# Changing the size of the first load, and with it the partition pitch, in a max-pooling kernel bound by its loads

## The chip, the cores and the metric

The kernel runs on one core of one Trainium2 chip. The metric is the device time of a run in microseconds (us); medians of several runs are given. The span in a profile is the same execution without what surrounds it, about 1.7 us less. On one core there is no second die to compare with, and all runs quoted here counted as fast runs, at a granted clock of 1.00.

## The reference

The reference takes x of 32 x 256 x 4096 float32 and gives 32 x 256 x 256: each output is the maximum of 16 neighbouring inputs.

```
for i in range(output_size):                 # 256
    start = int(i * length / output_size)    # 16 * i
    end = int((i + 1) * length / output_size)
    result[:, :, i] = np.max(x[:, :, start:end], axis=-1)
```

So 134.2 MB are read, 8.4 MB are written, and there is one operation: a maximum over windows of W = 16 elements (64 B). Each of the 128 partitions handles 16,384 windows.

## The kernel before

A partition reads consecutive windows from the input. The windows come in two groups; within a group, partition p starts p x (windows of the group) x 64 B behind the group's first byte. That distance is called the *pitch* here. One buffer, `ring`, has two halves, each with a gap of 152 windows, so that a load can be issued when the larger part (872 windows) of the reduction before it in the same half is done. The results go to a second buffer, `kept`, and leave at the end in two *kept stores*, one for each group. The results of the last load alone go to a free part of `ring` and leave in a transfer of their own, the *small store*, which ScalarE issues when the last reduction is done.

```
CHUNK = 1024
GAP = 152
FIRST = 132
LOADS_A, LOADS_B = 9, 6
last = total - FIRST - (LOADS_A + LOADS_B) * CHUNK      # 892
...
for g, loads in enumerate(
    ([FIRST] + [CHUNK] * LOADS_A, [CHUNK] * LOADS_B + [last])
):
    xg, og = group(sum(loads))       # [128 partitions, windows of the group]
    a = 0
    for n in loads:
        xn = xg[:, a * W : (a + n) * W]
        ...                          # FIRST goes into the gap, the rest:
        low = n_loads % 2 * (CHUNK + GAP)
        moved = n_loads // 2 % 2
        at = low + moved * GAP
        nc.sync.dma_start(out=ring[:, at * W : (at + n) * W], in_=xn)
        if n == CHUNK:
            cut = CHUNK - GAP if moved else GAP
            parts = [(0, cut), (cut, n)]
            for u, v in parts if moved else parts[::-1]:
                pooled(dst[:, u:v], at + u, v - u)     # reduce_max into kept
        else:
            end = (at + CHUNK) * W
            last_kept = ring[:, end - n : end]
            pooled(last_kept, at, n)
        ...
nc.scalar.dma_start(out=og[:, full : full + last], in_=last_kept)
tc.no_sync_barrier()
for dst, src in stores:              # one kept store for each group
    nc.sync.dma_start(out=dst, in_=src)
```

## Time and profile before

| | before |
|---|---|
| first three runs, median (lowest to highest) | 335.11 us (334.94 to 335.2) |
| span of the profiled run | 333.4 us |
| VectorE busy | 276.5 us, 83% |
| rate of an 8 MB load in the steady part | 433.5 GB/s |
| VectorE idle before each 8 MB load's reduction | 2.07 us |

The page's part on DMA issues, below, has in its columns the tile written and read, the issuing queue, the count, the size, and the time from issue to landing. In all profile lines DVE is VectorE, which does the reductions; SPq and ACTq are the queues of SyncE and ScalarE, which issue the transfers.

### The profile page before, as it was taken

The numbers are of one execution on the slowest core, as the hardware profiler recorded it, in microseconds if no ns is written. First come the engines' busy times: TensorE is split into PE (matmuls) and PEld (weight loads), VectorE is DVE, ScalarE is ACT, GpSimd is POOL, SyncE is SP. The second block draws the span as 40 slices with busy tenths as digits, with TensorE's granted clock in tenths as the row PEclk, the third lists the DMA queues.
The fourth block names the chain that finished last, engine by engine and source line by source line (L and its number), as shares of the span: only waits on it lengthen the run. The fifth ranks groups of instructions, "written<-read, shape, count | busy, mean of one in ns | idle before, by whom it ended". The sixth has DMA issues, their size and how long they took to land.

```text
span 333.4 us, 113 instructions
## 1 busy us (share of the span) xinstructions
DVE 276.5 (83%) x32; POOL 0.2 (0%) x4
## 2 busy tenths in 40 slices
DVE  2009979797997979799797979979797997979993
POOL 0000000000000000000000000000000000000000
DMA  9898989999898989999898989999898989899997
GB/s 381 377 503 377 495 385 480 401 401 480 377 503 377 503 377 480 401 393 488 377 503 377 503 377 480 401 425 456 377 503 377 503 377 495 385 455 438 397 402 317
DMA packets 2880, 142.61 MB, mean 428 GB/s; under 512 B 320, under 2 KB 320, under 8 KB 448
## 3 DMA queue, kind: packets, MB, share of 16 engines
q1 hardware_dynamic: 2736, 142.15, 98.7%
q10 hardware_dynamic: 144, 0.46, 0.3%
HBM read 134.22 MB, written 8.39 MB: 428 GB/s over the span
## 4 chain that ended last, share of the span: by engine, by line
DMA 58%; DVE 36%; DVEq 5%; issue 0%; SPq 0%
DMA ring<-in_x_dram 58%; DVE kept L52 36%; DVEq L143 5%; SPq L83 0%
## 5 line engine op out<-in xcount | busy, mean ns | idle before, releaser
L52 DVE TENSOR_REDUCE kept<-ring 128x872 f32<-128x13952 f32 (+2 forms) x31 | 261.5, 8477 | 51.8 <-DMA ring<-in_x_dram 51.8
L52 DVE TENSOR_REDUCE ring<-ring 128x892 f32<-128x14272 f32 x1 | 15.0, 15009 | 0.0
L129 POOL MEMSET const-bfloat16-1.0<- 128x1 bf16 x1 | 0.1, 102 | 0.0
L129 POOL MEMSET const-uint8-127<- 128x1 uint8 x1 | 0.1, 102 | 0.0
L129 POOL MEMSET const-float32-1.0<- 128x1 f32 x1 | 0.1, 99 | 0.0
L129 POOL MEMSET const-float32-0.0<- 128x1 f32 x1 | 0.1, 98 | 0.2 <-issue 0.2
## 6 DMA issues: line engine op xcount, KB each, us to landing
ring<-in_x_dram SPq DMA_DIRECT2D x1, 7136.0 KB, 21.5
out_dram<-kept SPq DMA_DIRECT2D x1, 4674.0 KB, 32.2
out_dram<-kept SPq DMA_DIRECT2D x1, 3072.0 KB, 18.0
ring<-in_x_dram SPq DMA_DIRECT2D x1, 1056.0 KB, 5.1
out_dram<-ring ACTq DMA_DIRECT2D x1, 446.0 KB, 4.2
ring<-in_x_dram SPq DMA_DIRECT2D x15, 24.0
```

Of the source, the lines that this page charges most:

```text
L52: nc.vector.reduce_max(out=dst, in_=ring[:, at * W : (at + n) * W].rearrange("p (n w) -> p n w", w=W), axis=mybir.AxisListType.X,)
L129: nc = _bacc.Bacc("TRN2", target_bir_lowering=False, num_devices=1)
L143: with _tile.TileContext(nc) as tc:
```

## The change

The first load becomes 128 windows, exactly 8 KB per partition, in place of 132 (8448 B). That alone would make the pitch of the first group an even number of 256 B (9344 x 64 = 2336 x 256 B), so the ninth 8 MB load is made 4 windows, 256 B, shorter: 2335 x 256 B. The last load takes the 8 windows left over, 900 in place of 892.

```
-    FIRST = 132
+    FIRST = 128
     LOADS_A, LOADS_B = 9, 6
-    last = total - FIRST - (LOADS_A + LOADS_B) * CHUNK
+
+    LESS = 4
+    group_a = [FIRST] + [CHUNK] * (LOADS_A - 1) + [CHUNK - LESS]
+    last = total - sum(group_a) - LOADS_B * CHUNK
+    group_b = [CHUNK] * LOADS_B + [last]
 ...
-    for g, loads in enumerate(
-        ([FIRST] + [CHUNK] * LOADS_A, [CHUNK] * LOADS_B + [last])
-    ):
+    for g, loads in enumerate((group_a, group_b)):
 ...
-                if n == CHUNK:
+                if n != last:
```

## The prediction

> **What bounds the kernel now.** I read the page's shares first, then the memory line, then the chain of waits, then the DMA queue's own waits, and last the stretches of the start and the end. The page says which resource is full:
>
> ```profile
> DVE 276.5 (83%) x32; POOL 0.2 (0%) x4
> DMA packets 2880, 142.61 MB, mean 428 GB/s; under 512 B 320, under 2 KB 320, under 8 KB 448
> q1 hardware_dynamic: 2736, 142.15, 98.7%
> HBM read 134.22 MB, written 8.39 MB: 428 GB/s over the span
> ```
>
> VectorE has 17% of slack, the DMA queue of SyncE has 1.3%. The reads are exactly the input (134.22 MB) and the writes exactly the output (8.39 MB), so no byte can be saved. The packet count also tells how a transfer is cut. There are 17 loads and 3 stores of 128 partitions, 20 x 128 = 2560 packets, and 20 x 16 = 320 small ones (the "under 512 B" group, the completion signals); together 2880. So each partition's run, 64 KB long or 8448 B long, is one packet.
>
> The chain of waits in order of time alternates between loads and reductions. Three of its pieces in the middle and all from the last wait on:
>
> ```profile
> 25.17 14.70 DVE kept L52
> 39.87 0.02 issue
> 39.88 23.97 DMA ring<-in_x_dram
> ...
> 272.09 23.96 DMA ring<-in_x_dram
> 296.06 0.02 issue
> 296.08 16.89 DVE kept L52 x2
> 312.97 0.09 issue
> 313.06 15.23 DVEq L143
> ```
>
> That looks as if each 14.7 us reduction were on the path, since the load is issued only when it ends. It is not. The 8 MB load issued at 39.88 needs only 19.35 us of transfer, yet takes 23.97 us, so it stands 4.6 us in the queue behind the load before it. VectorE's lines of the timeline near the end give that period, and the slack on the other side:
>
> ```profile
> 257.38 17.28 DVE L52 TENSOR_REDUCE kept<-ring 128x872 f32<-128x13952 f32 x2 [2.07 <-DMA ring<-in_x_dram]
> 276.74 17.28 DVE L52 TENSOR_REDUCE kept<-ring 128x872 f32<-128x13952 f32 x2 [2.08 <-DMA ring<-in_x_dram]
> 296.08 17.28 DVE L52 TENSOR_REDUCE kept<-ring 128x872 f32<-128x13952 f32 x2 [2.06 <-DMA ring<-in_x_dram]
> 313.27 15.01 DVE L52 TENSOR_REDUCE ring<-ring 128x892 f32<-128x14272 f32 x1
> ```
>
> Starts lie 19.35 us apart, work is 17.28 us, VectorE idles 2.07 us a round. A load of 128 x 65536 B = 8,388,608 B in 19.35 us is 433.5 GB/s: the loads run back to back at one rate and set the pace. At the end two paths nearly meet. VectorE goes on without a pause (296.08 + 17.28 = 313.36) into the last reduction and is done at 328.28, after which the last small store takes 4.2 us to land. The DMA engines meanwhile do the other two stores. The stretches show that they have no hole either:
>
> ```profile
> core 0: us, DVE busy (x) POOL busy (x), PEclk, DMA share, GB/s
> 5.86:8.21 2.35, 2.35 (x1) 0.00 (x0) 1.00 1.03 446
> 8.21:25.17 16.96, 0.00 (x2) 0.00 (x0) 1.00 1.00 433
> 25.17:313.27 288.10, 259.10 (x30) 0.00 (x0) 1.00 1.00 431
> 313.27:328.28 15.01, 15.01 (x2) 0.00 (x0) 1.00 1.01 436
> 328.28:333.36 5.08, 0.00 (x1) 0.00 (x0) 1.00 0.59 245
> ```
>
> The fourth row is the last reduction: DMA share 1.01, full, with stores of the kept results. In the trace's packet records the last kept-store packet ends 1.1 us before the last packet of the small store. So the span is: some 1.7 us until the first packet, 330.25 us in which the engines always have packets, and 1.4 us of receipt and closing. The timed run adds about 1.7 us to the span (335.11 against 333.4).
>
> **What the Trainium skill says.** "DMA: Bandwidth & Descriptors", section "Where 436 GB/s comes from", puts the ceiling of the 16 engines' way into SBUF at 435.2 GB/s. The trace agrees: 433.5 GB/s in the steady part, so no better layout in HBM can win more than 0.4%. The same page, section "How a descriptor splits into AXI transactions", says that a run aligned to 256 B is cut into transactions of 256 B and a remainder. The old first run is 8448 B = 33 x 256, the new one 8192 B = 32 x 256, and both start on a 256 B boundary (every load starts at a multiple of 4 windows of 64 B). By that section 8448 B has no remainder to lose; the trace shows it as one packet and at best 319 ns, 16 x 8448 / 319 = 424 GB/s, so hardly worse than a long one. The same page's "Latency and other measured facts" has a row on HBM row pitches at large powers of two that halve the rate; nothing of the kind is to be seen in this trace. "VectorE: DVE Perf Modes", in its perf-mode table, has tensor_reduce at 1x in fp32 only, with a clock of 0.96 GHz: 872 x 16 elements would be an estimate of 14.53 us, the trace has 14.69. So a window of 16 costs 16.8 ns (15,009 ns / 892).
>
> **The change part by part.** No operation is added or removed: 32 reductions, 17 loads, 3 stores as before, with the same waits in the built program. Only four sizes move.
>
> (1) First load 132 to 128 windows per partition. Removed: 128 x 256 B = 32,768 B, at 433.5 GB/s 0.076 us. The first reduction starts perhaps 0.08 us earlier and is 4 x 16.8 = 67 ns shorter. It has 16.96 us of idle time behind it, so nothing reaches the end from VectorE.
> (2) Ninth 8 MB load 1024 to 1020 windows: again 0.076 us less transfer, and its big reduction 872 to 868 windows, 67 ns less, in front of an idle 2.07 us. Hidden.
> (3) The last load takes what the two gave up, 892 to 900 windows: 65,536 B more, +0.151 us. Sum of the loads: -0.076 - 0.076 + 0.151 = 0.00 us, so the last load lands when it did. The load before it lands 0.15 us earlier.
> (4) The last reduction is 8 x 16.8 = 0.135 us longer. VectorE's tail: start of the last 17.28 us pair 0.151 us earlier, last reduction 0.135 us longer, sum -0.016 us. It ends at about 328.26 instead of 328.28, provided that the last load is there when VectorE becomes free. It lands at about 313.06 and VectorE comes free at 313.27 - 0.15 = 313.12: just in time; were it 0.1 us late, VectorE would end at 328.36. The small store grows from 3568 to 3600 B a partition, 4 KB or 0.01 us, and a kept store shrinks by as much.
>
> The pitch between partitions of the first group goes from 9348 x 64 = 598,272 B = 2337 x 256 B to 9340 x 64 = 597,760 B = 2335 x 256 B; of the second group from 7036 x 64 = 1759 x 256 B to 7044 x 64 = 1761 x 256 B. All four are odd, and counted in units of 8 KB they lie one 256 B step above or below a whole number (2336 = 73 x 32, 1760 = 55 x 32): the two groups only swap sides. I expect the same rate. Total: 0.00 us for the bytes, -0.02 to +0.1 us for the tail.
>
> **The rivals.** (a) *The start gains.* The first load needs 3.7 us from first to last packet where the steady rate would need 2.5, and single packets take up to 1186 ns. If exactly 8 KB avoided some of that, up to 1.2 us could go: 333.9. For it: those long packets. Against it: they are only the earliest ones, later packets of the same load take 319 ns, which is what start-up looks like, not a cost per packet. I give it one chance in ten for a part, 0.3 us. (b) *The pitch changes the rate.* If 2335 and 1761 suited HBM worse, the 8 MB packets, now about 2418 ns, would lengthen; 1% is 3.2 us: 338.3. Against it: mirror-image pitches. For it: somebody took pains to keep it odd. (c) *The last wait changes hands.* VectorE waits for the last load instead of for itself: at most +0.1 us: 335.2. Plausible, and hardly measurable beside a spread of 0.26 us between three runs. (d) *VectorE's tail gains because the work is better spread.* It cannot: the DMA queue is full to the end on its own.
>
> **Range and chances.** Bytes, packets and operations are the same, so the middle is 335.11 less a few hundredths, with a small pull from (a): 335.05. The three runs spread over 334.94 to 335.20; adding (a) and (c), and a different hour or chip, gives 334.6 to 335.6 for 8 in 10. To gain 2% (6.7 us) the 142.61 MB would have to go through in 330.25 - 6.7 = 323.5 us, that is at 441 GB/s where they now take 432, above anything steady here; to lose as much needs rival (b) at double size. Faster 0.01, same 0.98, slower 0.01.
>
> **What would show it right or wrong.** Right: the page again has 2880 packets, 142.61 MB and 428 GB/s; reductions of 8 MB loads start 19.35 us apart, except 0.08 us less around the ninth; the last reduction is about 15.14 us and begins about 313.1; the queue's share stays near 98.7%. Step (1) is wrong if the first reduction starts earlier than 5.5 us and the whole chain shifts with it. Rival (b) shows as a period other than 19.35 us; rival (c) as idle time before the last reduction. The prediction as a whole fails if the long packets' rate moves by even half a per cent, or if the packet count changes.

## More of the kernel before

The large times contain time in the queue, as the prediction works out for an 8 MB load.

```profile
ring<-in_x_dram SPq DMA_DIRECT2D x1, 7136.0 KB, 21.5
out_dram<-kept SPq DMA_DIRECT2D x1, 4674.0 KB, 32.2
out_dram<-kept SPq DMA_DIRECT2D x1, 3072.0 KB, 18.0
ring<-in_x_dram SPq DMA_DIRECT2D x1, 1056.0 KB, 5.1
out_dram<-ring ACTq DMA_DIRECT2D x1, 446.0 KB, 4.2
ring<-in_x_dram SPq DMA_DIRECT2D x15, 24.0
```

## The result, and the profile after

| | before | after |
|---|---|---|
| median of 6 runs each (lowest to highest) | 334.96 us (334.92 to 335.2) | 334.87 us (334.78 to 335.01) |
| ratio | | 0.9996, 95% interval 0.9984 to 1.0009 |
| span of the profiled run | 333.4 us | 333.2 us |

A ratio is the mean time of one kernel's fast runs over that of the other's of the same rounds, so it isn't quite the ratio of the two medians.

The page of the changed kernel, its parts on bytes and queues:

```profile
DVE 276.5 (83%) x32; POOL 0.2 (0%) x4
DMA packets 2880, 142.61 MB, mean 428 GB/s; under 512 B 320, under 2 KB 320, under 8 KB 448
q1 hardware_dynamic: 2736, 142.15, 98.8%
HBM read 134.22 MB, written 8.39 MB: 428 GB/s over the span
```

Packets, bytes and mean rate are those of before. VectorE's timeline of the changed kernel, its first two and last four lines (start, duration, operation, count, and the idle time ahead of it):

```profile
5.40 2.29 DVE L56 TENSOR_REDUCE kept<-ring 128x128 f32<-128x2048 f32 x1 [5.40 <-DMA ring<-in_x_dram]
24.75 17.28 DVE L56 TENSOR_REDUCE kept<-ring 128x872 f32<-128x13952 f32 x2 [17.07 <-DMA ring<-in_x_dram]
...
257.06 17.28 DVE L56 TENSOR_REDUCE kept<-ring 128x872 f32<-128x13952 f32 x2 [2.08 <-DMA ring<-in_x_dram]
276.41 17.28 DVE L56 TENSOR_REDUCE kept<-ring 128x872 f32<-128x13952 f32 x2 [2.07 <-DMA ring<-in_x_dram]
295.75 17.28 DVE L56 TENSOR_REDUCE kept<-ring 128x872 f32<-128x13952 f32 x2 [2.07 <-DMA ring<-in_x_dram]
312.95 15.14 DVE L56 TENSOR_REDUCE ring<-ring 128x900 f32<-128x14400 f32 x1
```

The period is still about 19.35 us (19.36 in the mean; single starts lie 19.24 to 19.47 us apart), and the last reduction took 15.14 us without idle time before it. But the whole column lies 0.22 to 0.46 us earlier than before (296.08 became 295.75; 25.17 became 24.75). The first lines of the same view of the kernel before show where that begins:

```profile
5.86 2.35 DVE L52 TENSOR_REDUCE kept<-ring 128x132 f32<-128x2112 f32 x1 [5.86 <-DMA ring<-in_x_dram]
25.17 17.28 DVE L52 TENSOR_REDUCE kept<-ring 128x872 f32<-128x13952 f32 x2 [16.96 <-DMA ring<-in_x_dram]
```

The first load landed 0.46 us earlier, 0.38 us more than the bytes account for. Of this 0.46 us only 0.17 us are left in the span. Two questions follow: whether the start is a property of 8 KB, and why VectorE's lead is not in the result. The second can in part be worked out from the lines. At the last pair, of the lead of 0.33 us, 0.15 us are the bytes taken from the first and the ninth load, and the last load takes them back; the other 0.18 us are about what the span has. The rest of the early lead was lost in single loads on the way (two starts of the changed kernel, 140.94 and 160.41, lie 19.47 us apart).

### The profile page after: what moved, and what is told of

It is laid out like the page before. It is cut to its first block, busy times and chain, and to the rows that moved or that the text cites. A ratio compares the mean times of both kernels' runs of the same rounds, so it can differ in the third digit from the quotient of the medians.

```text
span 333.2 us, 113 instructions
## 1 busy us (share of the span) xinstructions
DVE 276.5 (83%) x32; POOL 0.2 (0%) x4
## 2 busy tenths in 40 slices
DMA packets 2880, 142.61 MB, mean 428 GB/s; under 512 B 320, under 2 KB 320, under 8 KB 448
## 4 chain that ended last, share of the span: by engine, by line
DMA 57%; DVE 36%; DVEq 5%; issue 0%; SPq 0%
DMA ring<-in_x_dram 57%; DVE kept L56 36%; DVEq L145 5%; SPq L85 0%
## 5 line engine op out<-in xcount | busy, mean ns | idle before, releaser
L56 DVE TENSOR_REDUCE kept<-ring 128x152 f32<-128x2432 f32 (+3 forms) x31 | 261.4, 8473 | 51.6 <-DMA ring<-in_x_dram 51.6
L56 DVE TENSOR_REDUCE ring<-ring 128x900 f32<-128x14400 f32 x1 | 15.1, 15141 | 0.0
```

Of the source, the lines that this page charges most:

```text
L56: nc.vector.reduce_max(out=dst, in_=ring[:, at * W : (at + n) * W].rearrange("p (n w) -> p n w", w=W), axis=mybir.AxisListType.X,)
```

## The experiments

Eleven runs were made: eight new kernels, one of them three times (e1, e6, e11), and the changed kernel again (e7). e1 to e4 ran on one chip, e5 to e8 on a second, e9 to e11 on a third. The theory: the 16 DMA engines, full from the first packet to the last, set the time by bytes alone. Rivals: the reductions or VectorE's tail are on the path; exactly 8 KB starts faster; the pitch matters. "Before" stands for runs of the unchanged kernel in the same rounds.

| run | median, us | before, us | ratio | 95% interval |
|---|---|---|---|---|
| e1_even_pitch | 334.68 | 334.98 | 0.9993 | 0.9981 to 1.0006 |
| e2_first_8448 | 335.12 | 334.98 | 1.0003 | 0.9991 to 1.0016 |
| e3_first_4608 | 335.06 | 334.98 | 1.0003 | 0.9990 to 1.0016 |
| e4_half_reduce | 335.06 | 334.98 | 1.0004 | 0.9990 to 1.0017 |
| e5_extra_tail | 337.47 | 335.08 | 1.0073 | 1.0060 to 1.0086 |
| e6_even_again | 334.68 | 335.08 | 0.9987 | 0.9974 to 0.9999 |
| e7_after_again | 335.05 | 335.08 | 1.0000 | 0.9986 to 1.0014 |
| e8_one_group | 354.01 | 335.08 | 1.0564 | 1.0549 to 1.0578 |
| e9_shifted_store | 334.82 | 335.15 | 0.9990 | 0.9978 to 1.0003 |
| e10_even_less8 | 335.17 | 335.15 | 1.0000 | 0.9987 to 1.0012 |
| e11_even_third | 334.70 | 335.15 | 0.9986 | 0.9973 to 1.0000 |

All results were correct except those of e4 and e9.

### Is VectorE on the path at all? (e4)

```
-            in_=ring[...].rearrange("p (n w) -> p n w", w=W),
+            in_=ring[...].rearrange("p (n w) -> p n w", w=W)[:, :, 0 : W // 2],
```

> Wrong result on purpose: every reduction reads 8 of the 16 elements of a window, so VectorE has half the work (about 138 us) and all loads, stores and waits stay. Theory (loads run back to back at the engines' rate): period of 8 MB loads stays 19.35 us; only the tail can gain, since VectorE then ends some 16 us earlier: at most the 0.8 us in which the engines are not full at the end, 334.0 to 334.9. Rival (each reduction is on the path, as the chain of waits suggests with 36%): tens of us faster, below 300.

Measured: 335.06 us. VectorE's timeline of this run, near the end:

```profile
276.57 8.75 DVE L56 TENSOR_REDUCE kept<-ring 128x872 f32<-128x6976 f32 x2 [10.60 <-DMA ring<-in_x_dram]
295.92 8.75 DVE L56 TENSOR_REDUCE kept<-ring 128x872 f32<-128x6976 f32 x2 [10.61 <-DMA ring<-in_x_dram]
313.01 7.65 DVE L56 TENSOR_REDUCE ring<-ring 128x900 f32<-128x7200 f32 x1 [8.35 <-DMA ring<-in_x_dram]
```

Each pair of reductions takes 8.75 us in place of 17.28, and the idle time before it grows by as much: 276.57 to 295.92 is 19.35 us as ever. VectorE finished at 320.66 us, over 7 us earlier than in the changed kernel, and the time did not move; it is even just above the 334.0 to 334.9 expected, as an earlier end of VectorE gained nothing. So the 36% of the span that the chain of waits gives to reductions are not on the path, and neither is VectorE's tail. The DMA queue alone sets the end.

The trace's packet records agree. Adding up the time of all packets and dividing by 16 engines gives 330.30 us for the kernel before, 330.36 for the changed one and 330.46 here; from the first packet to the last there are 330.25, 330.09 and 330.23 us. The engines are full, whatever VectorE does.

### How much slack has VectorE's tail? (e3, e5)

e3 shortens the first load further, which lengthens the last one:

```
-    FIRST = 128
+    FIRST = 72          # 4608 B; the last load becomes 956 windows
```

> First load of 72 windows (4608 B, pitch odd again), last load 956 instead of 900. Theory (VectorE's tail and the DMA queue nearly tie at the end): VectorE is now free at about 311.9 us, waits for the last load until about 312.8, then reduces for 956 x 16.83 ns = 16.09 us until 328.85, 0.76 us later than in the changed kernel, and the small store ends the span: about 335.6. Rival (the DMA queue alone sets the end): 334.9. Rival (a shorter first load makes the start cheaper): below 334.8.

Measured: 335.06 us. The last reduction behaves as expected, the time does not: it did not rise to 335.6. The end of the timeline, and the small store's line in the part on DMA issues:

```profile
312.90 16.09 DVE L56 TENSOR_REDUCE ring<-ring 128x956 f32<-128x15296 f32 x1 [0.95 <-DMA ring<-in_x_dram]
```

```profile
out_dram<-ring ACTq DMA_DIRECT2D x1, 478.0 KB, 3.3
```

VectorE waits 0.95 us for the last load and ends at 328.99, 0.9 us later than in the changed kernel (328.09). But the small store now lands 3.3 us after its issue in place of 4.2, and takes the delay up. So the 4.2 us were not a fixed cost. They contain waiting behind the packets of the kept store. To find how much, e5 adds work that is known, in front of the last reduction:

```
+                    pooled(last_kept[:, 0:244], at, 244)
                     pooled(last_kept, at, n)
```

> The changed kernel with one reduction more, just ahead of the last one: 244 windows of the last load, 244 x 16.83 ns = 4.1 us, whose result the last reduction overwrites (the result stays right). It measures how much slack VectorE's tail has. Theory (the DMA queue ends the span; the small store's 4.2 us hold about 1 us of waiting behind the kept store, as 3.3 us in the run with a 4608 B first load suggest): the end moves by 4.1 - 1.0 = 3.1 us, about 338.0, and the small store lands 3.2 to 3.3 us after its issue. Rival (VectorE's tail and the DMA queue end together, no slack, as predicted): +4.1 us, 339.0. Rival (VectorE never matters): 334.9.

Measured: 337.47 us, against 335.05 for the changed kernel in the same rounds (e7): +2.42 us. The end of this run, first the stores, then the stretches (time, DVE busy and count, POOL, clock, DMA share, GB/s):

```profile
out_dram<-kept SPq DMA_DIRECT2D x1, 3072.0 KB, 18.1
...
out_dram<-ring ACTq DMA_DIRECT2D x1, 450.0 KB, 2.5
```

```profile
328.00:330.00 2.00, 2.00 (x1) 0.00 (x0) 1.00 0.92 393
330.00:331.00 1.00, 1.00 (x1) 0.00 (x0) 1.00 0.01 0
331.00:332.00 1.00, 1.00 (x1) 0.00 (x0) 1.00 0.00 0
332.00:333.00 1.00, 0.26 (x1) 0.00 (x0) 1.00 0.00 0
```

The changed kernel's small store and the same two stretches, for comparison:

```profile
out_dram<-ring ACTq DMA_DIRECT2D x1, 450.0 KB, 4.2
```

```profile
330.00:331.00 1.00, 0.00 (x0) 0.00 (x0) 1.00 0.57 227
331.00:332.00 1.00, 0.00 (x0) 0.00 (x0) 1.00 0.59 234
```

In e5 the DMA engines are empty from about 330.6 us on while VectorE still works: the tail has become the path. The small store was issued at 332.29 in place of 328.13 us (e7), 4.16 us later, and the time rose by 2.42: the slack is 4.16 - 2.42 = 1.7 us. The store says the same: alone it lands after 2.5 us, in the changed kernel after 4.2, a difference of 1.7. I had expected 1.0.

### Does exactly 8 KB start faster? (e2)

```
-    FIRST = 128
+    FIRST = 132
-    LESS = 4
+    LESS = 8            # pitch and last load as in the changed kernel
```

> First load back to 132 windows (8448 B), ninth load 1016 windows instead of 1020, so that pitch and last load are those of the changed kernel: undoes the 8 KB alone. Theory (bytes only change place): 334.9, within 0.15 of the changed kernel; the first reduction starts at 5.4 to 5.9 us whatever the size. Rival (exactly 8 KB starts faster, first reduction at 5.40 against 5.86 us): first reduction near 5.86 and the time 335.2 to 335.3.

Measured: 335.12 us, with the first reduction at 5.56 us. With 8192 B it began at 5.40 (after), 5.50 (e1), 5.37 (e4), 5.45 (e5), 5.51 (e6), 5.48 (e7), 5.51 (e9), 5.60 (e10) and 5.43 us (e11), and at 6.42 with the pitch of e8; with 8448 B at 5.86 (before) and 5.56 (e2). The 256 B should cost about 0.08 us, and 5.56 lies within the scatter of the others; the other 0.3 us of the kernel before are in that one profile only, and there is no second one of it. Whether the 8 KB are worth a tenth of a microsecond is not resolved: the changed kernel had a median of 334.87 in its first rounds and 335.05 in e7, and this run's time is above both, between what the theory and the rival expected; its ratio to the kernel before, 1.0003, lies inside the 95% intervals of both (0.9984 to 1.0009, and 0.9986 to 1.0014). The first load's packets show no jump at 8 KB: in the median a packet of 8448 B took 319 ns (before) and one of 8192 B 309 ns (after), in proportion to their bytes.

### Does the odd pitch matter? (e1, e6, e11, e8)

e1, e6 and e11 are one kernel, the first half of the change without the second; e7 is the changed kernel unaltered:

```
-    LESS = 4
+    LESS = 0            # pitches 73 x 8 KB and 55 x 8 KB
```

> The first load of 8192 B alone, without the shortened ninth load: the pitch between partitions becomes 9344 x 64 = 2336 x 256 B = 73 x 8 KB in the first group and 1760 x 256 B = 55 x 8 KB in the second, so all partitions of a group start at the same place modulo 8 KB. Theory (the rate is set by the 16 engines, not by the layout in HBM): period of the 8 MB loads stays 19.35 us, time 334.9 within 0.3. Rival (the odd pitch is what keeps the rate, as the change's own words say): the packets of 64 KB, now 2418 ns, lengthen and the period exceeds 19.4 us; 1% would be 338.

> The even pitch (multiples of 8 KB) once more, beside the changed kernel on the same chip, as it came out 0.2 us below it in different rounds. Theory (the pitch does nothing here, the differences are chance): 334.7 to 335.0, within 0.15 of the changed kernel. Rival (an even pitch is a little better): again 0.2 us or more below the changed kernel in the same rounds.

> The kernel with the pitch of 73 x 8 KB a third time, as yardstick of these rounds. Theory (a small but real gain): 334.55 to 334.8, below the kernel before by 0.3 us. Rival (chance in two sets of rounds): 334.9 to 335.1.

> The changed kernel, unaltered, as the yardstick of these rounds. Every theory: 334.87 within 0.15.

Measured: 334.68, 334.68 and 334.70 us, and 335.05 for the changed kernel beside the second. So the pitch that the change avoids costs nothing. It is even a little better: in 15 runs the kernel with pitches of a multiple of 8 KB took 334.54 to 334.93 us, against 334.78 to 335.34 for the changed kernel in 11. In the rounds that they shared (e6 and e7) all five of its runs are below all five of the changed kernel's, as the rival of e6 expected. That is 0.1%, and only repetition makes it visible.

e8 shows that a pitch *can* cost. It makes one group of the two, so the pitch is 16,384 x 64 B = 1 MiB:

```
-    for g, loads in enumerate((group_a, group_b)):
+    for g, loads in enumerate((group_a + group_b,)):
...
+        one = sum(group_a)          # the kept store is cut where it was
+        stores.append((og[:, 0:one], kept[:, 0:one]))
+        stores.append((og[:, one:full], kept[:, one:full]))
```

> One group instead of two: every partition reads one run of 16384 windows, so the pitch between partitions is 1,048,576 B, a power of two, instead of an odd number of 256 B; loads, reductions and bytes are the same, and the kept store is cut at the same place (its pitch in the output becomes 64 KB). Theory of the layout's author[...]: packets of 64 KB become much longer than 2418 ns, half rate would be about 640 us. Theory that the 16 engines alone set the rate whatever the pitch: 334.9 within 1.

Measured: 354.01 us, 5.6% more. Its page and four lines of VectorE's timeline:

```profile
DMA packets 2880, 142.61 MB, mean 404 GB/s; under 512 B 320, under 2 KB 320, under 8 KB 448
```

```profile
233.59 17.28 DVE L56 TENSOR_REDUCE kept<-ring 128x872 f32<-128x13952 f32 x2 [3.54 <-DMA ring<-in_x_dram]
253.14 17.28 DVE L56 TENSOR_REDUCE kept<-ring 128x872 f32<-128x13952 f32 x2 [2.27 <-DMA ring<-in_x_dram]
274.16 17.28 DVE L56 TENSOR_REDUCE kept<-ring 128x872 f32<-128x13952 f32 x2 [3.74 <-DMA ring<-in_x_dram]
293.84 17.28 DVE L56 TENSOR_REDUCE kept<-ring 128x872 f32<-128x13952 f32 x2 [2.40 <-DMA ring<-in_x_dram]
```

With the same packets and bytes, starts now lie 19.3 to 22.5 us apart over the whole run, and between loads VectorE idles up to 5.24 us. The records have the 64 KB load packets at 2539 ns in the mean (2422 in the changed kernel). The median is 2418 ns in both: most packets are as fast as before, but 27% took more than 2500 ns (1% in the changed kernel), up to 4082 ns. From the first packet to the last it takes 19.5 us more; 14.8 us per engine of that are longer packets, the rest is time without any. The store packets, whose pitch in the output also became a power of two (64 KB), stayed at 912 and 1382 ns. So it is the reads that are slower. It is a loss of 5.6%, neither the halving that one theory expected nor the nothing of the other: both missed.

### What is the 0.3 us of the multiple of 8 KB? (e9, e10)

With 9344 and 7040 windows the output rows start at multiples of 256 B too. e9 keeps the loads and moves the stores by 16 B; e10 takes pitches that are even but no multiple of 8 KB, with output rows off 256 B.

```
e9, from the kernel of e1:
-        stores.append((og[:, 0:full], kept[:, base : base + full]))
+        cols = full if g else full - 4
+        stores.append((og[:, 4 : 4 + cols], kept[:, base : base + cols]))
   (the small store likewise, 4 outputs further on)
e10, from the changed kernel:
-    LESS = 4
+    LESS = 8            # pitches 2334 x 256 B and 1762 x 256 B
```

> Wrong result on purpose: the kernel with the pitch of 73 x 8 KB (first load 8192 B, ninth load not shortened), with every store moved by 4 outputs, that is 16 B, in the output, and two of them 16 B a row shorter. Loads, waits and reductions are those of the kernel with the even pitch, whose output rows all start at multiples of 256 B (9344 x 4 = 146 x 256). Theory (the 0.3 us between that kernel and the changed one come from output rows off 256 B boundaries, which cost the stores and what runs beside them): 334.9 to 335.1, store packets back to the sizes of the changed kernel. Rival (they come from the pitch of the input, which is even): 334.68 as before, within 0.1.

> First load 8192 B, ninth load 1016 windows: pitch 9336 x 64 = 2334 x 256 B and 7048 x 64 = 1762 x 256 B, both even, but output rows of 37,344 and 28,192 B that are not multiples of 256 B. Theory (alignment of the output rows): 334.9 to 335.1 like the changed kernel. Rival (an even pitch of the input is what gains): 334.7.

Measured: 334.82 and 335.17 us, beside 334.70 for the multiple of 8 KB in the same rounds. An even pitch alone gains nothing (e10). Moving the stores lost 0.12 us of the 0.45 us between that kernel and the one before in these rounds (335.15): less than the theory of the stores expected (334.9 to 335.1), and about the 0.1 us that its rival allowed. Its store packets took 19.49 us per engine, against 19.48 for the aligned one and 19.51 to 19.52 in the two traces of the changed kernel, which is too little to explain even this. So alignment of the output is at most a part; what else a pitch of a multiple of 8 KB helps is left open, and so is whether 8 KB is the measure: the pitches of e10 are odd multiples of 512 B, and no run has one between 512 B and 8 KB. In the traces of the changed kernel (after, e7) the packets of the last load ran longer than 2418 ns for 64 KB by 0.18 and 0.32 us per engine, in those of the 8 KB multiple (e1, e6, e11) by 0.04, 0.06 and 0.10 us. But e4 and e5, with the pitch of the changed kernel, have 0.10, and the kernel before 0.05, so this isn't tied to the pitch.

## Why the prediction was right or wrong

**The time** was right: 334.87 us, predicted 335.05 with a range of 334.6 to 335.6; the later rounds gave 335.05.

**What bounds it** was right, and more strictly than it said: at the end VectorE's tail had time to spare. The loads run back to back, and the period of 19.35 us survived halving all reductions (e4).

**Parts (1) to (3)**, bytes that change place and sum to nothing, were right: 142.61 MB and 2880 packets again, and the same time.

**Part (4)**, the tail, had the right sizes: the last reduction took 15.14 us as worked out, and VectorE had no idle time before it, so rival (c) did not show in this profile. (The prediction's 313.36 for the end of the pair before it lies 0.08 us after the shown start, 313.27: the records of successive reductions overlap by that.) In the second profile of the changed kernel, e7, the last reduction began 0.01 us after the end of the pair, and 0.05 us after the wait for the last load, so there rival (c) may hold the 0.1 us that it was given. The tail's end at 328.09 in place of 328.26 comes from the shift of the whole column. What was wrong is the step before it, "At the end two paths nearly meet". It took the 4.2 us from the small store's issue to its landing for a cost of its own. Alone the store lands after 2.5 us (e5); 1.7 us are waiting behind the kept store. So VectorE's tail has 1.7 us of slack, and none of the -0.02 to +0.1 us from it could have reached the time. This did no harm here because the terms were small. With a change that lengthened the tail by 4 us it would have been wrong by the whole slack.

**The test for step (1)** fired: the first reduction began at 5.40 us, below the 5.5 set, and the column shifted with it. The test was badly set, since other runs with 8192 B show 5.37 to 5.60 us, and the time doesn't follow them: e4 began at 5.37 us and had a span of 333.5 us, e1 at 5.50 and 332.9. Of rival (a) nothing is shown; an effect of a tenth of a microsecond stays unresolved.

**Rival (b)**, the pitch, was rightly held unlikely for mirror-image pitches, but its ground, that an odd pitch is worth keeping, was taken over from the change without proof. The pitch of a multiple of 8 KB costs nothing and was in three sets of rounds 0.3 to 0.45 us better than the kernel before. The pitch of 1 MiB costs 19 us.

## What to carry to other kernels

Here the transfer engines were full from the first packet to the last, and moving bytes between loads changed nothing beyond 0.14 us against the kernel before (e2, e3); add up the packets' time and compare it with the span before tuning sizes. The time from issue to landing of the last store can contain waiting behind other stores (1.7 of 4.2 us here), so it is no cost to add to a compute tail: measure it alone, or add known work and see how much of it comes through. And a rule about layout ("keep the pitch odd") is to be tested by breaking it: here the variant without the second half of the change was at least as fast, and of the pitches tried only the power of two, 1 MiB, was slow.

## What the Trainium skill lacked or had wrong

- "DMA: Bandwidth & Descriptors", section "Latency and other measured facts": for rows of 16 KiB copied between HBM tensors, the row on HBM row pitches gives 207 GB/s at 512 KiB, 164 at 2 MiB and 214 at a padded pitch, and nothing for 1 MiB. Here, with loads into SBUF of up to 64 KB per partition and a pitch of 1 MiB, the loss was 5.6% (404 GB/s over the span in place of 428).
- No page compares pitches that are no large power of two. Here, near 600 and 450 KB, odd multiples of 256 B and even ones gave 335 us, multiples of 8 KB 334.7 us.
- "DMA: Bandwidth & Descriptors", section "SWDGE vs HWDGE vs iDMA", has "≤4096 B preferably" for a packet, in a table about transfers that GpSimd issues. For those that SyncE and ScalarE issue, as all do here, it gives no size. The traces record each partition's run of up to 64 KB as one packet (2880 packets for 142.61 MB).
- No page says how much of a small store's time is waiting in the queues: 450 KB landed 2.5 us after issue when alone, and 4.2 us when issued some 2.6 us before the last packet of a larger store ended.
